# A hybrid decoder layer on one core: the first half of weight block 0 in two transfers of 256 columns, 256-wide first products, one warm-up product less

## The chip, the cores and the metric

The kernel runs on one core of a Trainium2 chip. The metric is device time in microseconds (us) for one execution; the time before is the median of three runs. Engines are named as the profile names them: PE (TensorE; PEld are its weight loads), DVE (VectorE), ACT (ScalarE), POOL (GpSimd), and SP (SyncE, which only issues transfers here). ACT issues a few transfers too; ACTq and SPq stand for the two queues.

## The reference

One decoder layer on 256 tokens of width 1024, all in float32: an input projection into two head groups (block-sparse attention and retention) with an output projection, cross-attention into a memory of 256 tokens, and a gated feed-forward block. Each has a normalised input and a normalised output that is added to x. Only the beginning matters here, the input projection:

```python
def rms_norm(x, g):
    xf = x.astype(jnp.float32)
    y = xf * lax.rsqrt(jnp.mean(xf * xf, axis=-1, keepdims=True) + NORM_EPS)
    return (y * g.astype(jnp.float32)).astype(x.dtype)
...
        h = rms_norm(x, g_pre_mix[l])
        proj = h @ w_in[l]
        mq, mk, mv, rq, rk, rv, rg = jnp.split(proj, SPLIT_POINTS, axis=-1)
```

## The kernel before

Every product is made of float32 operands split in two: a high part rounded to the matrix format (fp32r) and a low part, the rest. A product of x and w is then three products, high x with high w, low x with high w, high x with low w, all summed in one accumulator bank of 512 columns. The token-side scale of the norm is applied after the product, the gain before it.

The weights come in blocks of 128 x 1024 (512 KB) that SP loads in order of use into one of six `raw` tiles (`load_weight`, L149 to 157). ACT rounds a block into the high part (L197) and DVE subtracts for the low part (L198); both go into one of nine `hl` tiles. TensorE walks through a list of steps written out ahead, each with its products; side work is resumed between steps.

The opening is written out by hand, ahead of that list:

- TensorE starts with `WARM` products of constants (L999 and L1000), which feed nothing.
- ACT issues the transfer of the first half of block 0 (columns 0 to 511 of `raw0`, L989), then part 1 of x (`xr0`, L991), and loads its function table (L992).
- SP issues `xg` (L1014: the gains and part 0 of x), the second half of block 0 (L1015), the two halves of block 1 (L1016, L1017), parts 2 and 3 of x (L1018), and then whole blocks (L157).
- x is stored transposed in eight parts of 128 rows by 256 tokens. `gain_split` scales a part with the gain and rounds it on ACT (L230: high part of `xT`), then DVE makes the low part (L231).
- Block 0 has its own splitting (L1067 to 1078): DVE rounds the first half (L1074, CAST in the profile), ACT the second (L1077), DVE makes both low parts (L1078). Block 1 is split in halves by `split_weight(1, 2)`, after ACT has rounded part 1 of x.
- The first eight steps ("first", L1107 to 1116) multiply part q of x with half c of block q, q from 0 to 3. Each makes six products of 512 columns: three pairs of parts, each for both halves of the tokens. From block 4 on, steps are of the kind "col" (L1117 to 1133), with weights laid out in another way and the same three products (L1128 to L1130).

Transfers share eight completion counters (DMAHW0 to DMAHW7 in the order of instructions), given out in turn. A transfer that reuses a counter is issued only after the one before it on that counter has landed. A tile's reader waits for the transfer of just the columns that it reads.

Of the kernel before, what the change touches and what calls it, by code (L numbers as in the profile page):

```python
# [7 lines left out]
F32 = mybir.dt.float32  # L8
F32R = mybir.dt.float32r
BF16 = mybir.dt.bfloat16  # L10
AF = mybir.ActivationFunctionType
ALU = mybir.AluOpType
AX = mybir.AxisListType

P = 128
D = 1024
# [31 lines left out]
WARM = 9  # L48
# [7 lines left out]
def tile_hybrid_layer(  # L56
# [14 lines left out]
    nc = tc.nc  # L71
# [15 lines left out]
    def tok(t):  # L87
        return slice(t * P, (t + 1) * P)
# [33 lines left out]
    T = {}  # L122
# [866 lines left out]
    nc.scalar.dma_start(raws[0][:, 0:512], weights[0, :, 0:512])  # L989
    xr = [p4.tile([P, 4, 256], F32, tag="p4", name=f"xr{i}") for i in range(2)]  # L990
    nc.scalar.dma_start(xr[0][:, 1, :], gx[:, 288:544])  # L991
    nc.scalar.preload_act_table(AF.Exp)  # L992
# [20 lines left out]
    raws[1] = rawp.tile([P, D], F32, tag="raw", name="raw1")  # L1013
    nc.sync.dma_start(xg, gx[:, 0:288])  # L1014
    nc.sync.dma_start(raws[0][:, 512:1024], weights[0, :, 512:1024])  # L1015
    nc.sync.dma_start(raws[1][:, 0:512], weights[1, :, 0:512])  # L1016
# [54 lines left out]
    for c in range(2):  # L1071
        n = slice(c * 512, (c + 1) * 512)
        if c == 0:
            nc.vector.tensor_copy(hls[0][:, 0, n], raw[:, n])  # L1074
            gain_split("xT", 0, xg[:, 32:288], 0)
        else:
            nc.scalar.activation(hls[0][:, 0, n], raw[:, n], AF.Copy)  # L1077
        nc.vector.tensor_tensor(out=hls[0][:, 1, n], in0=raw[:, n], in1=hls[0][:, 0, n].bitcast(F32), op=ALU.subtract)  # L1078
# [9 lines left out]
    for i, s in enumerate(steps):  # L1088
# [17 lines left out]
        if s[0] == "first":  # L1106
# [4 lines left out]
            for a, (hx, hw) in enumerate(((0, 0), (1, 0), (0, 1))):  # L1111
                for t in range(2):
                    begin = q == 0 and a == 0
                    if begin:
                        accs[(c, t)] = accS(f"acc{c}{t}")
                    nc.tensor.matmul(accs[(c, t)], T["xT"][:, hx, q, tok(t)], h[:, hw, :], start=begin, stop=False)  # L1116
        elif s[0] == "col":  # L1117
# [5 lines left out]
            for kk in range(2):  # L1123
                k = 2 * kp + kk
                need((st, k, t))
                xh = T[st][:, 0, k, tok(t)]
                xl = T[st][:, 1, k, tok(t)]
                nc.tensor.matmul(acc, xh, h[:, 0, kk, :], start=(first and kk == 0), stop=False)  # L1128
                nc.tensor.matmul(acc, xh, h[:, 1, kk, :], start=False, stop=False)  # L1129
                nc.tensor.matmul(acc, xl, h[:, 0, kk, :], start=False, stop=(last and kk == 1))  # L1130
# [195 lines left out]
```

## Time and profile before

| what | value |
| --- | --- |
| median of 3 runs | 398.45 us |
| the three runs | 398.23, 398.45, 400.76 us |
| profiled execution | 398.61 us |
| its span, first to last instruction | 396.8 us |
| mean granted TensorE clock | 0.997 |
| bytes read from memory | 79.02 MB |

The span is what the profile covers, and the profiled execution's own time holds 1.8 us more around it. The trace gives starts and durations in us from the span's start. A row of the timeline or of the chain reads: start, duration, engine, line, operation, tiles written and read, shape, count, and in brackets how long the engine was idle before and what released it. A row of the view of waits reads: who waited, for whom, us in total, times, longest. In a table of issues the columns are tile, engine, count, KB each, and us from the issue to the landing. A row of grouped instructions has us busy and mean ns of one after the bar. Rows of stretches give busy us (and instructions) for PE, PEld, DVE, ACT and POOL, then the granted clock, the busy share of the 16 DMA engines, and GB/s.

### The profile page before, as it was taken

Reading aid. Unit: us, or ns where it says so; the run is one execution under the profiler, and the core shown is the slowest. Engines: PE = TensorE matmul, PEld = TensorE weight load, DVE = VectorE, ACT = ScalarE, POOL = GpSimd, SP = SyncE. Lnnn points to the kernel's source line nnn. Section 1 sums busy time; section 2 is a strip of 40 time slices with the busy share of each in tenths; the row PEclk is TensorE's granted clock in tenths of the full one; section 3 lists DMA queues with packets and bytes.
Section 4 is the critical chain, followed back from the end, with each engine's and each line's share of the span. In section 5 each row is a group of like instructions: output and inputs, shape, how many; then the busy total and the mean of one; then the engine's idle time right before and its main releaser. Section 6 shows DMA issues by size and latency. Waiting matters only on the chain.

```text
span 396.8 us, 5496 instructions
## 1 busy us (share of the span) xinstructions
PE 389.1 (98%) x1975; PEld 324.1 (82%) x1975; DVE 321.6 (81%) x448; ACT 259.7 (65%) x436; POOL 33.3 (8%) x53
## 2 busy tenths in 40 slices
PE   8999999999999999999999999999999999999993
PEld 4888787888889888888888888888888888888883
DVE  4865976785869977577576699999899799999964
ACT  5785965954767865494546866766758685656741
POOL 0010020200011000000001001013113103101000
PEclk9999999999999999999999999999999999999998
DMA  8998845568547676607272559779939878954102
GB/s 279 413 402 262 272 121 196 160 188 297 172 152 243 175 223 194 215 10 243 68 265 57 156 192 356 249 155 314 272 95 293 225 238 189 355 198 73 36 0 106
DMA packets 23067, 80.42 MB, mean 203 GB/s; under 512 B 2560, under 2 KB 3200, under 8 KB 23040
## 3 DMA queue, kind: packets, MB, share of 16 engines
q1 hardware_dynamic: 18144, 62.91, 46.6%
q0 software_dynamic: 4608, 16.78, 17.2%
q10 hardware_dynamic: 288, 0.39, 0.3%
q8 instruction: 15, 0.25, 0.3%
q14 instruction: 12, 0.10, 0.1%
HBM read 79.02 MB, written 1.05 MB: 202 GB/s over the span
## 4 chain that ended last, share of the span: by engine, by line
PE 89%; DVE 4%; ACT 3%; issue 2%; DMA 1%; POOLq 0%; POOL 0%; DVEq 0%; ACTq 0%
PE x L1192 11%; PE acc L1128 11%; PE acc L1129 10%; PE acc L1130 10%; PE acc L1152 9%; PE y L1192 5%; PE acc L1155 5%; PE down L1175 5%; PE down L1177 5%; PE down L1176 5%; PE acc L1116 3%; PE z L1192 3%; DVE hl L198 1%; ACT p_m L313 1%; DMA raw<-in_weights_dram 1%
## 5 line engine op out<-in xcount | busy, mean ns | idle before, releaser
L198 DVE TENSOR_TENSOR hl<-raw,hl 128x1024 fp32r<-128x1024 f32 (+1 forms) x102 | 119.4, 1188 | 16.9 <-ACT hl L197 16.6
L197 ACT ACTIVATE hl<-raw 128x1024 fp32r<-128x1024 f32 (+1 forms) x102 | 102.5, 1032 | 1.1 <-DMA raw<-in_weights_dram 0.9
L197 ACT ACTIVATE hl<-sum_qv 128x1024 fp32r<-128x1024 f32 x22 | 23.0, 1056 | 15.2 <-DVE sum_qv L204 12.2
L1128 PE MATMUL acc<-hl,xT 128*128 128x512 f32 x80 | 32.9, 411 | 0.1
L1175 PE MATMUL down<-hl,fT 128*128 128x512 f32 (+1 forms) x84 | 32.0, 381 | 0.0
L1176 PE MATMUL down<-hl,fT 128*128 128x512 f32 (+1 forms) x84 | 31.9, 380 | 0.0
L1177 PE MATMUL down<-hl,fT 128*128 128x512 f32 (+1 forms) x84 | 31.9, 380 | 0.0
L1130 PE MATMUL acc<-hl,xT 128*128 128x512 f32 x80 | 31.3, 392 | 0.0
L1129 PE MATMUL acc<-hl,xT 128*128 128x512 f32 x80 | 31.3, 391 | 0.0
L198 DVE TENSOR_TENSOR hl<-sum_kT,hl 128x1024 fp32r<-128x1024 f32 x24 | 29.0, 1220 | 1.4 <-ACT hl L197 1.3
L197 ACT ACTIVATE hl<-sum_kT 128x1024 fp32r<-128x1024 f32 x24 | 24.8, 1050 | 5.4 <-DVE sum_kT L204 3.5
L198 DVE TENSOR_TENSOR hl<-sum_qv,hl 128x1024 fp32r<-128x1024 f32 x22 | 26.6, 1218 | 1.3 <-ACT hl L197 1.3
L1192 PE MATMUL x<-hl,comb 128*128 128x512 f32 x96 | 23.2, 391 | 0.0
L1192 PE MATMUL x<-hl,x2T 128*128 128x512 f32 x96 | 23.2, 393 | 0.0
L1192 PE MATMUL y<-hl,comb 128*128 128x512 f32 x96 | 23.1, 389 | 0.0
L1192 PEld LDWEIGHTS x<-hl,comb 128*128 128x128 f32 x96 | 17.9, 188 | 4.0 <-DVE hl L198 0.3
L1192 PEld LDWEIGHTS y<-hl,comb 128*128 128x128 f32 x96 | 18.0, 188 | 3.7
L1192 PEld LDWEIGHTS x<-hl,x2T 128*128 128x128 f32 x96 | 17.8, 188 | 3.7
L1177 PEld LDWEIGHTS down<-hl,fT 128*128 128x128 f32 x84 | 15.8, 188 | 3.1 <-DVE fT L667 0.2
L1175 PEld LDWEIGHTS down<-hl,fT 128*128 128x128 f32 x84 | 15.8, 188 | 2.9
L1176 PEld LDWEIGHTS down<-hl,fT 128*128 128x128 f32 x84 | 15.8, 188 | 2.9
L1128 PEld LDWEIGHTS acc<-hl,xT 128*128 128x128 f32 x80 | 15.0, 188 | 3.8 <-issue 0.7
(257 smaller groups left out, 863.1 us busy)
## 6 DMA issues: line engine op xcount, KB each, us to landing
raw<-in_weights_dram SPq DMA_DIRECT2D x98, 512.0 KB, 4.9
sum_kT<-in_weights_dram POOLq DMA_DIRECT2D x14, 512.0 KB, 7.0
sum_qv<-in_weights_dram POOLq DMA_DIRECT2D x10, 512.0 KB, 5.8
sum_ret<-in_weights_dram POOLq DMA_DIRECT2D x8, 512.0 KB, 4.9
gpost<-in_gpost_dram SPq DMA_DIRECT2D x3, 512.0 KB, 4.5
x_sb<-in_x_dram SPq DMA_DIRECT2D x2, 512.0 KB, 8.2
memn<-in_mem_dram SPq DMA_DIRECT2D x2, 512.0 KB, 5.9
mr<-in_memT_dram SPq DMA_DIRECT2D x2, 512.0 KB, 7.4
```

The costliest lines, as they stand in the source:

```text
L197: nc.scalar.activation(h[:, 0, n], raw[:, n], AF.Copy)
L198: nc.vector.tensor_tensor(out=h[:, 1, n], in0=raw[:, n], in1=h[:, 0, n].bitcast(F32), op=ALU.subtract)
L1116: nc.tensor.matmul(accs[(c, t)], T["xT"][:, hx, q, tok(t)], h[:, hw, :], start=begin, stop=False)
L1128: nc.tensor.matmul(acc, xh, h[:, 0, kk, :], start=(first and kk == 0), stop=False)
L1129: nc.tensor.matmul(acc, xh, h[:, 1, kk, :], start=False, stop=False)
L1130: nc.tensor.matmul(acc, xl, h[:, 0, kk, :], start=False, stop=(last and kk == 1))
L1152: nc.tensor.matmul(acc, hls[q][:, 0, k * P:(k + 1) * P], T[f"{st}_k"][:, k, :], start=begin, stop=end, skip_group_check=True)
L1155: nc.tensor.matmul(acc[:, 0:256], hls[q][:, 1, k * P:(k + 1) * P], T[st][:, 0, k, :], start=begin, stop=end, skip_group_check=True)
L1175: nc.tensor.matmul(bank, fh, wh, start=first, stop=False, skip_group_check=True)
L1176: nc.tensor.matmul(bank, fh, wl, start=False, stop=False, skip_group_check=True)
L1177: nc.tensor.matmul(bank, fl, wh, start=False, stop=last, skip_group_check=True)
L1192: nc.tensor.matmul(acc, a, h[:, w, kk, :], start=begin and kk == 0 and n == 0, stop=end and n == 2, skip_group_check=True)
```

## The change

The transfer of the first half of block 0 is cut in two. Columns 0 to 255 stay first on ACT's queue; columns 256 to 511 become the second transfer on SP's queue, ahead of the second half. Block 1's first half moves from SP's queue to ACT's, as its third transfer. DVE rounds only columns 0 to 255, and ACT rounds columns 256 to 511; each piece has its low part made by itself. The first step's six products become ten: columns 0 to 255 with high and low weights, columns 256 to 511 with high weights, then low x with the high weights of all 512 columns, then columns 256 to 511 with low weights. `WARM` falls from 9 to 8. The "col" branch is written as a loop over the same three products.

```diff
-WARM = 9
+WARM = 8
...
-    nc.scalar.dma_start(raws[0][:, 0:512], weights[0, :, 0:512])
+    nc.scalar.dma_start(raws[0][:, 0:256], weights[0, :, 0:256])
     xr = [p4.tile([P, 4, 256], F32, tag="p4", name=f"xr{i}") for i in range(2)]
     nc.scalar.dma_start(xr[0][:, 1, :], gx[:, 288:544])
+    raws[1] = rawp.tile([P, D], F32, tag="raw", name="raw1")
+    nc.scalar.dma_start(raws[1][:, 0:512], weights[1, :, 0:512])
     nc.scalar.preload_act_table(AF.Exp)
...
-    raws[1] = rawp.tile([P, D], F32, tag="raw", name="raw1")
     nc.sync.dma_start(xg, gx[:, 0:288])
+    nc.sync.dma_start(raws[0][:, 256:512], weights[0, :, 256:512])
     nc.sync.dma_start(raws[0][:, 512:1024], weights[0, :, 512:1024])
-    nc.sync.dma_start(raws[1][:, 0:512], weights[1, :, 0:512])
     nc.sync.dma_start(raws[1][:, 512:1024], weights[1, :, 512:1024])
...
-    for c in range(2):
-        n = slice(c * 512, (c + 1) * 512)
-        if c == 0:
-            nc.vector.tensor_copy(hls[0][:, 0, n], raw[:, n])
-            gain_split("xT", 0, xg[:, 32:288], 0)
-        else:
-            nc.scalar.activation(hls[0][:, 0, n], raw[:, n], AF.Copy)
-        nc.vector.tensor_tensor(out=hls[0][:, 1, n], in0=raw[:, n], in1=hls[0][:, 0, n].bitcast(F32), op=ALU.subtract)
+    hi, lo = hls[0][:, 0], hls[0][:, 1]
+
+    def low_part(a, b):
+        nc.vector.tensor_tensor(out=lo[:, a:b], in0=raw[:, a:b], in1=hi[:, a:b].bitcast(F32), op=ALU.subtract)
+
+    nc.vector.tensor_copy(hi[:, 0:256], raw[:, 0:256])
+    low_part(0, 256)
+    gain_split("xT", 0, xg[:, 32:288], 0)
+    nc.scalar.activation(hi[:, 256:512], raw[:, 256:512], AF.Copy)
+    low_part(256, 512)
+    nc.scalar.activation(hi[:, 512:1024], raw[:, 512:1024], AF.Copy)
+    low_part(512, 1024)
...
-            for a, (hx, hw) in enumerate(((0, 0), (1, 0), (0, 1))):
+            if q == 0:
                 for t in range(2):
-                    begin = q == 0 and a == 0
-                    if begin:
-                        accs[(c, t)] = accS(f"acc{c}{t}")
-                    nc.tensor.matmul(accs[(c, t)], T["xT"][:, hx, q, tok(t)], h[:, hw, :], start=begin, stop=False)
+                    accs[(c, t)] = accS(f"acc{c}{t}")
+            a, b = slice(0, 256), slice(256, 512)
+            whole = slice(0, 512)
+            passes = [(0, 0, whole), (1, 0, whole), (0, 1, whole)]
+            if (q, c) == (0, 0):
+                passes = [(0, 0, a), (0, 1, a), (0, 0, b), (1, 0, whole), (0, 1, b)]
+            for hx, hw, n in passes:
+                for t in range(2):
+                    nc.tensor.matmul(accs[(c, t)][:, n], T["xT"][:, hx, q, tok(t)], h[:, hw, n],
+                                     start=(q == 0 and hx == 0 and hw == 0 and n is not b), stop=False, skip_group_check=True)
```

The first products on TensorE before: the last warm-up product, then the first step (accumulators `acc00` and `acc01`, one for each half of the tokens) up to the second step's `acc10`. In brackets stands the engine whose work a product waits for.

```order
L1000 MATMUL warm_105<-const-bfloat16-1.0 128x512
L1116 MATMUL acc00_155<-hl0_133,xT_118 128x512 [waits DVE_49,Activation_49]
L1116 MATMUL acc01_157<-hl0_133,xT_118 128x512
L1116 MATMUL acc00_155<-hl0_133,xT_118 128x512 [waits DVE_49]
...
L1116 MATMUL acc10_170<-hl0_133,xT_118 128x512 [waits Activation_49]
L1116 MATMUL acc11_172<-hl0_133,xT_118 128x512
```

The same place on TensorE now:

```order
L1002 MATMUL warm_107<-const-bfloat16-1.0 128x512
L1126 MATMUL acc00_157<-hl0_133,xT_119 128x256 [waits DVE_49,Activation_49]
L1126 MATMUL acc01_158<-hl0_133,xT_119 128x256
L1126 MATMUL acc00_157<-hl0_133,xT_119 128x256 [waits DVE_49]
...
L1126 MATMUL acc00_157<-hl0_133,xT_119 128x256 [waits Activation_49]
...
L1126 MATMUL acc00_157<-hl0_133,xT_119 128x512 [waits DVE_49]
L1126 MATMUL acc01_158<-hl0_133,xT_119 128x512
...
L1126 MATMUL acc10_176<-hl0_133,xT_119 128x512 [waits Activation_49]
L1126 MATMUL acc11_177<-hl0_133,xT_119 128x512
```

The low weights of columns 0 to 255 moved up to second place, and a wait for ACT (columns 256 to 511) came in at third place.

ACT's first instructions before: two transfers, the table load, then x and weights in turn.

```order
L989 DMA raw0_99<-in_weights_dram 128x512
L991 DMA xr0_101<-in_gx_dram 128x256
L992 ACT_TABLE_LOAD
L230 ACTIVATE xT_118<-xg_94 128x256 [waits DMAHW1_49]
L1077 ACTIVATE hl0_133<-raw0_99 128x512 [waits DMAHW2_49]
L230 ACTIVATE xT_118<-xr0_101,xg_94 128x256 [waits DMAHW3_49]
L197 ACTIVATE hl1_144<-raw1_120 128x512 [waits DMAHW4_49]
```

The same place on ACT now:

```order
L989 DMA raw0_99<-in_weights_dram 128x256
L991 DMA xr0_101<-in_gx_dram 128x256
L993 DMA raw1_104<-in_weights_dram 128x512
L994 ACT_TABLE_LOAD
L230 ACTIVATE xT_119<-xg_94 128x256 [waits DMAHW1_49]
L1080 ACTIVATE hl0_133<-raw0_99 128x256 [waits DMAHW3_49]
L1082 ACTIVATE hl0_133<-raw0_99 128x512 [waits DMAHW5_49]
L230 ACTIVATE xT_119<-xr0_101,xg_94 128x256 [waits DMAHW2_49]
L197 ACTIVATE hl1_146<-raw1_104 128x512 [waits DMAHW4_49]
```

A third transfer came in ahead of the table load, and a 256-wide rounding between x and the second half of block 0; the work behind it stands one place later.

SP's first instructions before:

```order
L1014 DMA xg_94<-in_gx_dram 128x288
L1015 DMA raw0_99<-in_weights_dram 128x512
L1016 DMA raw1_120<-in_weights_dram 128x512
L1017 DMA raw1_120<-in_weights_dram 128x512
L1018 DMA xr0_101<-in_gx_dram 128x512
L157 DMA raw2_126<-in_weights_dram 128x1024
L157 DMA raw3_128<-in_weights_dram 128x1024 [waits DMAHW0_49]
L1022 DMA xr1_102<-in_gx_dram 128x1024 [waits DMAHW1_49]
```

The same place on SP now:

```order
L1015 DMA xg_94<-in_gx_dram 128x288
L1016 DMA raw0_99<-in_weights_dram 128x256
L1017 DMA raw0_99<-in_weights_dram 128x512
L1018 DMA raw1_104<-in_weights_dram 128x512
L1019 DMA xr0_101<-in_gx_dram 128x512
L157 DMA raw2_126<-in_weights_dram 128x1024 [waits DMAHW0_49]
L157 DMA raw3_128<-in_weights_dram 128x1024 [waits DMAHW1_49]
L1023 DMA xr1_102<-in_gx_dram 128x1024 [waits DMAHW2_49]
```

The second half of block 0 went from second to third place, block 1's first half left the queue, and since eight transfers now go out ahead of block 2 instead of seven, block 2 waits for counter 0, which is that of the first weight transfer.

More of the change, by code (lines that the diff above doesn't have):

```diff
@@ L1127, in tile_hybrid_layer @@
                 xl = T[st][:, 1, k, tok(t)]
-                nc.tensor.matmul(acc, xh, h[:, 0, kk, :], start=(first and kk == 0), stop=False)
-                nc.tensor.matmul(acc, xh, h[:, 1, kk, :], start=False, stop=False)
-                nc.tensor.matmul(acc, xl, h[:, 0, kk, :], start=False, stop=(last and kk == 1))
+                for n, (a, w) in enumerate(((xh, 0), (xh, 1), (xl, 0))):
+                    nc.tensor.matmul(acc, a, h[:, w, kk, :], start=(first and kk == 0 and n == 0),
+                                     stop=(last and kk == 1 and n == 2), skip_group_check=True)
             if last:
```

## The prediction

> **What bounds the kernel now.** I read the page's busy shares and its chain by engine first, to see which engine a shift must go through. The profiled execution took 398.61 us: its span of 396.8 us and 1.8 us around it. It lies 0.16 us above the median of the runs shown, 398.45; the sum below is made against the profiled execution, and its difference is then put on the median.
>
> ```profile
> span 396.8 us, 5496 instructions
> PE 389.1 (98%) x1975; PEld 324.1 (82%) x1975; DVE 321.6 (81%) x448; ACT 259.7 (65%) x436; POOL 33.3 (8%) x53
> PE 89%; DVE 4%; ACT 3%; issue 2%; DMA 1%; POOLq 0%; POOL 0%; DVEq 0%; ACTq 0%
> ```
>
> TensorE is busy 98% of the span and carries 89% of the chain that ended last. So the opening is worth what it does to the time at which TensorE is through with it; from there a shift goes almost one for one to the end. Next the view of waits, for PE and its weight loads:
>
> ```profile
> PE acc L1116 <- DVE hl L1074: 0.8, 1, 0.8
> ...
> PEld acc L1116 <- ACT xT L230: 1.6, 1, 1.6
> ...
> PEld acc L1128 <- ACT rvd L242: 0.3, 1, 0.3
> ...
> PEld acc L1116 <- DVE hl L1078: 0.2, 1, 0.2
> ```
>
> The reader is to see that the first product has two gates which open almost together: the rounded weights (CAST, L1074) and the rounded x (L230). After it, the only wait of the opening is 0.2 us for the low part of the weights, and the largest later one 0.3 us, so little could swallow a shift. Then the timeline of the first microseconds (start, duration, engine, line; ACTq and SPq are transfers being issued):
>
> ```profile
> 0.74 0.41 ACTq L989 DMA_DIRECT2D raw<-in_weights_dram  x1
> 0.74 0.38 SPq L1014 DMA_DIRECT2D xg<-in_gx_dram  x1
> 0.78 4.00 PE L1000 MATMUL warm<-const-bfloat16-1.0 128*128 128x512 bf16 x9 [0.78 <-PEq L1316]
> 1.18 0.45 ACTq L991 DMA_DIRECT2D xr<-in_gx_dram  x1
> 1.18 0.42 SPq L1015 DMA_DIRECT2D raw<-in_weights_dram  x1
> 1.65 0.42 SPq L1016 DMA_DIRECT2D raw<-in_weights_dram  x1
> 1.66 1.28 ACT L992 ACT_TABLE_LOAD   x1 [1.66 <-PEq L1316]
> 2.12 0.43 SPq L1017 DMA_DIRECT2D raw<-in_weights_dram  x1
> 3.06 0.71 SPq L157 DMA_DIRECT2D raw<-in_weights_dram  x1
> 4.78 0.51 ACT L230 ACTIVATE xT<-xg 128x256 fp32r<-128x256 f32 x1 [1.84 <-DMA xg<-in_gx_dram]
> 4.96 0.43 DVE L1074 CAST hl<-raw 128x512 fp32r<-128x512 f32 x1 [4.96 <-DMA raw<-in_weights_dram]
> 5.33 0.48 DVE L231 SCALAR_TENSOR_TENSOR xT<-xg,xT 128x256 fp32r<-128x256 f32 x1
> 5.50 0.76 PEld L1116 LDWEIGHTS acc<-hl,xT 128*128 128x128 f32 x4 [1.64 <-ACT xT L230]
> 5.54 11.18 PE L1116 MATMUL acc<-hl,xT 128*128 128x512 f32 x48 [0.76 <-DVE hl L1074]
> 5.88 0.63 ACT L1077 ACTIVATE hl<-raw 128x512 fp32r<-128x512 f32 x1 [0.59 <-DMA raw<-in_weights_dram]
> 16.56 0.39 PE L1128 MATMUL acc<-hl,xT 128*128 128x512 f32 x1
> 22.00 0.39 PE L1128 MATMUL acc<-hl,xT 128*128 128x512 f32 x1
> ```
>
> And the issues with the us to landing (one view for each stretch in which they were issued; xg and the 4.2 one at 0.74, the 4.9 and 4.7 ones at 1.18, then 1.65, 2.12 and 3.06):
>
> ```profile
> xg<-in_gx_dram SPq DMA_DIRECT2D x1, 144.0 KB, 4.0
> raw<-in_weights_dram ACTq DMA_DIRECT2D x1, 256.0 KB, 4.2
> xr<-in_gx_dram ACTq DMA_DIRECT2D x1, 128.0 KB, 4.9
> raw<-in_weights_dram SPq DMA_DIRECT2D x1, 256.0 KB, 4.7
> ...
> raw<-in_weights_dram SPq DMA_DIRECT2D x1, 256.0 KB, 5.0
> ...
> raw<-in_weights_dram SPq DMA_DIRECT2D x1, 256.0 KB, 5.2
> ...
> raw<-in_weights_dram SPq DMA_DIRECT2D x1, 512.0 KB, 6.2
> ```
>
> Issue plus landing time gives the landings: xg 4.74, first half of block 0 4.93; second half of block 0 5.88, xr 6.08; first half of block 1 6.65, its second half 7.32; block 2 9.26. Two things follow. The last two halves land 0.67 us apart, so 256 KB cost 0.67 us once the queues run full. And the heads of the two queues land in pairs: 144 KB on SP with 256 KB on ACT (0.19 us apart), then 256 KB on SP with 128 KB on ACT (0.20 us apart). The smaller one is not ahead by its size. The nth transfer of one queue thus lands with the nth of the other, whatever its bytes.
>
> Last, the pace: 24 products from 16.56 to 22.00 are 5.44/24 = 0.227 us for one 512 wide. Blocks 1 to 3 have 36 such products before 16.56, so block 1 begins at 16.56 - 36 x 0.227 = 8.39. That time is what the change can move.
>
> **The change, step by step.**
>
> *First product.* Its gate of weights opens earlier, but the gate of x stays: xT's rounding ends at 4.78 + 0.51 = 5.29 and the weight load starts 0.21 later, at 5.50. Halving the ACT transfer alone would gain 5.54 - 5.50 = 0.04 us. What can gain more is that xg shares its way with 128 KB less. Bounds: nothing, and 128 KB at the pace above, 0.33 us. I take 0.30, since the pair lands together: xg at 4.44, first product at 5.24. CAST and low part of 256 columns follow their own landing (about 4.6) and fit ahead: for the nearest rows,
>
> ```profile
> L540 ACT ACTIVATE ckh<-kf 128x256 fp32r<-128x256 f32 x8 | 3.4, 430 | 0.2 <-DVE kf L741 0.2
> ...
> L541 DVE TENSOR_TENSOR ckl<-kf,ckh 128x256 fp32r<-128x256 f32 x8 | 3.3, 416 | 0.0
> ...
> 113.15 1.91 PE acc L1155 x16
> ```
>
> a 256-wide rounding on ScalarE takes 0.43 us, a low part on VectorE 0.42, and a 256-wide product 1.91/16 = 0.119 (chain of waits, whole group of 16). Even with a CAST of the full old 0.43 the low part ends at 4.6 + 0.43 + 0.42 = 5.45, by the third product (5.24 + 2 x 0.119 = 5.48) give or take 0.15.
>
> *Ten products in place of six.* 8 x 0.119 + 2 x 0.227 = 1.41 us against 6 x 0.227 = 1.36: 0.05 us, although each 256-wide product brings its own weight load.
>
> *Columns 256 to 512.* Their transfer is now the second on SP. The bytes through the second pair are 144 + 128 + 128 + 128 = 528 KB; before, 400 KB were there at 4.93 and 784 KB at 6.08, so between them 5.31. ScalarE rounds in 0.43 and TensorE starts some 0.2 later: 5.31 + 0.43 + 0.2 = 5.94, where TensorE would be ready at 5.24 + 4 x 0.119 = 5.72. A wait of 0.22 us, which takes the place of the old 0.2 us one. The group then ends at 5.94 + 4 x 0.119 + 2 x 0.227 = 6.87. The low part of these columns (0.42 us after 5.74) is there by 6.3, ahead of its products.
>
> *Columns 512 to 1024.* This is the step that decides. Their transfer was second on SP and is now third, and beside it, third on ACT, now runs block 1's first half. Bytes through the third pair: 528 + 256 + 256 = 1040 KB. The same 1040 KB were there before at 6.65 (block 1's first half). So the landing lies between 5.88, as before, and 6.65; I take 6.5, near the pair's end, for the pairing above. Rounding 0.63 and 0.2 to the first product: 7.33. TensorE is ready at 6.87 and waits 0.46 us; six products later, at 7.33 + 1.36 = 8.69, block 1 begins, against 8.39 before: **0.30 us later**. With a landing at 5.88 the rounding is through at 5.88 + 0.83 = 6.71; TensorE is ready at 6.87, or at 5.24 + 1.41 = 6.65 if columns 256 to 512 cost no wait, so block 1 begins between 8.07 and 8.23: 0.16 to 0.32 us earlier. With 6.65 it is 6.65 + 0.83 + 1.36 = 8.84: 0.45 us later.
>
> *Behind it.* ScalarE's x part 1 (0.5 us) and block 1's first half (0.63) follow the late rounding: 7.13 + 0.5 + 0.63 + 0.2 = 8.46, 0.2 us ahead of TensorE; VectorE's low parts are asked for only two to four products after that. One warm-up product less lies in idle time of TensorE. ACT's third issue (0.45, as its row for xr) moves the table load to end at 3.4, a microsecond before ScalarE is wanted. SP issues as many transfers as before, but block 2's issue, at 3.06, now waits for the first weight transfer (its counter is shared, see the order): about 4.65. With 4.0 us, the shortest landing seen, it lands at 8.65, and it did not land before 9.26 anyway, held by the bytes ahead. Nothing is paid.
>
> *Sum.* Profiled execution 398.61 + 0.30 = 398.9; on the median, 398.45 + 0.30 = 398.75, rounded to 398.8.
>
> **A clock that is not up yet.** Warm-up products come at a slower pace:
>
> ```profile
> 2.02 0.15 PEld L1000 LDWEIGHTS <-const-bfloat16-1.0 128*128 128x128 bf16 x1 [0.28 <-issue]
> ...
> 3.72 0.15 PEld L1000 LDWEIGHTS <-const-bfloat16-1.0 128*128 128x128 bf16 x1 [0.28 <-issue]
> ...
> 2.00:3.00 1.00, 1.00 (x4) 0.42 (x3) 0.00 (x0) 0.94 (x1) 0.00 (x0) 1.00 0.75 181
> ```
>
> Four steps from 2.02 to 3.72 are 0.425 us each for 512 columns, against 0.227 later; yet the clock column (1.00, third from the right) shows nothing of it. So the array rose from half pace between 3.72 and 5.54. Nine warm-ups keep it busy for 9 x 0.425 = 3.8 us, eight for 3.4. If eight don't suffice, the opening's products run at half pace for a while. The Trainium skill, "TensorE: Matmul & The Clock Gate", section "What's actually happening", says that a free-running window of about 3.4 us must have been busy before the clock is granted in full. By that, eight warm-ups would just fill one window that happened to begin with them, and nine have 0.4 us to spare; the trace of before fits it and can't show the threshold.
>
> **The rivals.**
>
> *Faster: the second half of block 0 isn't held up.* If the SP queue keeps its pace beside a third ACT transfer, block 1 begins 0.16 to 0.32 us earlier: 398.2. For it speaks that the DMA engines were only 0.75 busy from 2 to 3 us (second number from the right in the row above), so that more could run beside; against it, the pairing of landings. It decides if columns 512 to 1024 land before 8.39 - 1.36 - 0.83 = 6.2.
>
> *Slower: half pace in the opening.* Take the rise late by one run of nine warm-ups, 3.8 us from 5.24 to 9.04. The first group costs 8 x 0.213 + 2 x 0.425 = 2.55 and ends at 7.79, past the late rounding, whose wait vanishes. In the second group 3 products fall before 9.04 and 3 after: 3 x 0.425 + 3 x 0.227 = 1.96; block 1 begins at 9.75, 1.36 us later: 399.8. It decides if products after the first still come 0.2 us apart at 256 columns. Against it: in the trace the pace had risen by 5.54 with 0.8 us of idle time ahead of it.
>
> *Nothing happens.* xg lands at 4.74 again, and so does all else: the first product moves 0.04 us, and the time stays at 398.4. For it speaks that xg is its own transfer, first on its queue, and untouched.
>
> **How the numbers follow.** Forecast (0.1 to 0.45 us later) 0.5; faster rival 0.22; nothing 0.1; half pace 0.15; 0.03 for what I don't see. The range reaches from the faster rival at its bound (398.1), less the 0.2 us by which the fastest run lies under the median, to the half-pace rival (399.8) and the 0.16 us between profile and median: 397.9 to 400.0. 1% is 4.0 us, about what a measurement here can tell from no change, and no case comes near it in either direction: faster 0.01, same 0.97, slower 0.02.
>
> **What would show it.** In the profile after: xg landing near 4.4 and the first product near 5.24 (else the first term is wrong); ScalarE waiting for raw until about 6.5 ahead of the 512-wide rounding, and TensorE waiting some 0.46 us for it (else the pairing is); 256-wide products 0.12 us apart (0.21 is the half-pace rival); block 1 at 8.7. It is wrong as a whole if the time leaves the range while block 1 begins between 8.1 and 9.75: then the shift was not passed on one for one.

## The result and the profile after

The changed kernel took 401.23 us in the median of eight executions (400.32 to 402.39), the kernel before 398.51 us in eight beside it (398.04 to 400.76). The ratio is 1.0063, with a 95% interval of 1.004 to 1.0085: the change makes the kernel slower, by 2.7 us, where 0.3 us was forecast. The time lies outside the predicted range (397.9 to 400.0), though within 1%. The profiled execution took 400.46 us, 1.85 more than that of before.

The head of the page and its chain by engine, of the kernel after:

```profile
span 398.7 us, 5506 instructions
...
PE 388.7 (98%) x1978; PEld 324.4 (81%) x1978; DVE 321.4 (81%) x449; ACT 259.9 (65%) x437; POOL 33.3 (8%) x53
...
PE 88%; DVE 4%; ACT 3%; issue 2%; DMA 1%; SPq 0%; POOLq 0%; POOL 0%; DVEq 0%; ACTq 0%
```

TensorE has 0.4 us less work than before and yet the span is 1.9 us longer: the loss is waiting, not work. The view of waits, for PE and its weight loads:

```profile
PE acc L1126 <- ACT hl L1082: 1.9, 1, 1.9
...
PE acc L1126 <- ACT xT L230: 0.6, 1, 0.6
...
PEld acc L1126 <- ACT hl L1082: 2.1, 1, 2.1
```

One wait stands out, for ACT's rounding of columns 512 to 1024 (L1082). The timeline of the opening says why:

```profile
1.65 0.42 SPq L1017 DMA_DIRECT2D raw<-in_weights_dram  x1
1.65 0.45 ACTq L993 DMA_DIRECT2D raw<-in_weights_dram  x1
...
3.95 0.51 ACT L230 ACTIVATE xT<-xg 128x256 fp32r<-128x256 f32 x1 [0.53 <-DMA xg<-in_gx_dram]
4.13 0.29 DVE L1077 CAST hl<-raw 128x256 fp32r<-128x256 f32 x1 [4.13 <-DMA raw<-in_weights_dram]
...
4.57 1.81 PE L1126 MATMUL acc<-hl,xT 128*128 128x256 f32 x10 [0.62 <-ACT xT L230]
4.63 0.42 ACT L1080 ACTIVATE hl<-raw 128x256 fp32r<-128x256 f32 x1 [0.17 <-DMA raw<-in_weights_dram]
...
7.58 0.63 ACT L1082 ACTIVATE hl<-raw 128x512 fp32r<-128x512 f32 x1 [2.54 <-DMA raw<-in_weights_dram]
...
8.26 0.96 PE L1126 MATMUL acc<-hl,xT 128*128 128x512 f32 x3 [1.88 <-ACT hl L1082]
...
17.90 6.28 PE L1140 MATMUL acc<-hl,xT 128*128 128x512 f32 x27
```

The first product starts at 4.57, 0.97 us earlier than before (5.54), and the ten products of the first step are through at 6.38. Then nothing until 8.26, because ACT is idle for 2.54 us ahead of L1082, waiting for the transfer. The first product of the "col" steps, which stood at 16.56, stands at 17.90: 1.34 us later. Two issues at the same moment, 1.65, carry it; in the view of issues (KB each, us to landing) they are

```profile
raw<-in_weights_dram SPq DMA_DIRECT2D x1, 256.0 KB, 5.9
raw<-in_weights_dram ACTq DMA_DIRECT2D x1, 256.0 KB, 6.1
```

Columns 512 to 1024 land at 1.65 + 5.9 = 7.55, block 1's first half at 7.75: a pair, as forecast, but the first of them 0.9 us later than the upper bound of 6.65. The DMA engines' busy share and GB/s (the last two numbers) of two stretches, in the kernel after:

```profile
3.50:5.50 2.00, 1.38 (x8) 0.86 (x7) 1.33 (x4) 0.93 (x2) 0.00 (x0) 1.00 0.53 160
5.50:7.50 2.00, 0.89 (x6) 0.58 (x4) 0.12 (x1) 0.00 (x0) 0.00 (x0) 1.00 1.00 330
```

and in the kernel before:

```profile
3.50:5.50 2.00, 1.28 (x3) 0.15 (x1) 0.54 (x2) 0.51 (x1) 0.00 (x0) 1.00 0.97 350
5.50:7.50 2.00, 1.97 (x9) 1.54 (x10) 1.86 (x4) 1.62 (x4) 0.00 (x0) 1.00 1.05 397
```

From 3.5 to 5.5 us the engines were full before and are half idle in this execution. From 3.5 to 7.5 us they moved 2 x 350 + 2 x 397 = 1494 KB before and 2 x 160 + 2 x 330 = 980 KB after.

The rest of the loss lies at the other end of the kernel. The chain's piece called "issue 4.78", in which TensorE finishes the last products, starts 1.38 us later, but the span is 1.9 us longer. SP's waits from 390 us on, before:

```profile
SPq L1322 <- DMA out_dram<-x_sb: 1.4, 2, 1.1
```

and after:

```profile
SPq L1333 <- DMA out_dram<-x_sb: 1.8, 1, 1.8
```

What SP does at that line behind the last such wait (semaphore instructions, their durations in ns, first and last start), before:

```profile
L1322 SPq EVENT_SEMAPHORE  x3: 17/17/28, 395.9 to 396.8; - x3
```

and after:

```profile
L1333 SPq EVENT_SEMAPHORE  x10: 17/28/28, 397.3 to 398.6; - x10
```

At the end SP waits for the transfers' eight counters one after another. The transfers take the counters in turn, and the kernel after has one transfer more in all. Before, the last output transfer sat on the counter that is waited for last, so that the other seven were passed during its flight. After, it sits on an earlier one, and seven more instructions come behind its landing. From the start of the issue of the last output transfer to the start of SP's last instruction, just before the span ends, pass 3.14 us before and 3.58 after: 0.44 us. With 1.38 that makes 1.82 of the 1.85 us between the two profiled executions.

### The profile page after: what moved, and what is told of

Same layout as the page of the kernel before. It is cut to its first block, busy times and chain, and to the rows that moved or that the text cites. A ratio compares the mean times of both kernels' runs of the same rounds, so it can differ in the third digit from the quotient of the medians.

```text
span 398.7 us, 5506 instructions
## 1 busy us (share of the span) xinstructions
PE 388.7 (98%) x1978; PEld 324.4 (81%) x1978; DVE 321.4 (81%) x449; ACT 259.9 (65%) x437; POOL 33.3 (8%) x53
## 4 chain that ended last, share of the span: by engine, by line
PE 88%; DVE 4%; ACT 3%; issue 2%; DMA 1%; SPq 0%; POOLq 0%; POOL 0%; DVEq 0%; ACTq 0%
PE acc L1140 31%; PE x L1203 11%; PE acc L1163 9%; PE y L1203 5%; PE acc L1166 5%; PE down L1188 5%; PE down L1186 5%; PE down L1187 5%; PE z L1203 3%; PE acc L1126 2%; DMA raw<-in_weights_dram 1%; DVE hl L198 1%; ACT p_m L313 1%; PE c_f L664 1%; ACT hl L197 1%
## 5 line engine op out<-in xcount | busy, mean ns | idle before, releaser
L1140 PE MATMUL acc<-hl,xT 128*128 128x512 f32 x240 | 59.4, 398 | 0.1
L1140 PEld LDWEIGHTS acc<-hl,xT 128*128 128x128 f32 x240 | 43.8, 188 | 9.8 <-issue 0.7
L1140 PE MATMUL acc<-hl,memT 128*128 128x512 f32 x96 | 23.0, 392 | 0.0
L1140 PE MATMUL acc<-hl,oT 128*128 128x512 f32 x96 | 22.9, 392 | 0.0
L1140 PE MATMUL acc<-hl,x2T 128*128 128x512 f32 x96 | 22.5, 392 | 0.0
L1140 PE MATMUL acc<-hl,mixT 128*128 128x512 f32 x96 | 22.2, 390 | 0.0
L1140 PEld LDWEIGHTS acc<-hl,mixT 128*128 128x128 f32 x96 | 17.9, 188 | 3.9 <-issue 0.2
L1140 PEld LDWEIGHTS acc<-hl,x2T 128*128 128x128 f32 x96 | 17.9, 188 | 3.7
```

Of the source, the lines that this page charges most:

```text
L1140: nc.tensor.matmul(acc, a, h[:, w, kk, :], start=(first and kk == 0 and n == 0), stop=(last and kk == 1 and n == 2), skip_group_check=True)
```

## The experiments

The theory is that the late landing of columns 512 to 1024, held up by the third transfer on ACT's queue, is the main loss. Its rival puts the loss on the clock: eight warm-up products in place of nine. Later came two more questions, what the additional transfer costs at the end, and what about the third ACT transfer delays the landing. All times are medians beside the kernel before on the same chip.

**Nine warm-ups again.** The kernel after with

```diff
-WARM = 8
+WARM = 9
```

> The changed kernel with nine warm-up products again. If the loss beyond the profiled opening comes from the clock falling during TensorE's long wait for columns 512 to 1024, the ninth product, which lies ahead of that wait, changes nothing: 401.2 us within 0.5, and single runs still spread over 2 us. If the missing product itself is the cause, the time comes back by 0.8 us or more, to 400.4 or below, with runs close together.

400.68 us (400.26 to 401.23, 4 executions) against 398.25, ratio 1.0058 [1.0043, 1.0073]. The time lies between the two expectations, and the runs spread over 1 us, not 2. Of the 2.7 us 2.4 stay: the warm-up is not the main part of the loss. Columns 512 to 1024 land at 1.64 + 5.8 = 7.44. Whether the ninth product gives something back can't be told, since its profiled execution began at half pace all the same. Its stretches for PE (busy us and products, clock, DMA share, GB/s):

```profile
6.50:7.50 1.00, 1.00 (x5) 1.00 0.95 326
7.50:8.50 1.00, 1.00 (x4) 1.00 0.92 336
8.50:9.50 1.00, 1.00 (x3) 1.00 0.97 381
9.50:10.50 1.00, 1.00 (x6) 1.00 1.03 360
```

Four and then three products in a us that was busy throughout, then six: TensorE was at half pace until about 9.5. That is the half-pace rival of the prediction, with nine warm-ups, and as worked out there the wait for the late rounding vanishes behind it.

**Block 1's first half back on SP.** The kernel after, with this transfer in fourth place on SP:

```diff
-    nc.scalar.dma_start(raws[1][:, 0:512], weights[1, :, 0:512])
...
     nc.sync.dma_start(raws[0][:, 512:1024], weights[0, :, 512:1024])
+    nc.sync.dma_start(raws[1][:, 0:512], weights[1, :, 0:512])
```

> The changed kernel with block 1's first half back on SP's queue (xg, columns 256 to 511, columns 512 to 1023, then block 1). Theory 1 (the third transfer of a queue reaches the DMA engines late, and the narrow transfers ahead of it are through too soon to cover that): columns 512 to 1024 land no earlier than 6.9, TensorE waits over 1.2 us, 400 us or more. Theory 2 (block 1's half on ACT takes half of the bandwidth): they land by 6.2, TensorE waits under 0.4 us, 398.5 us or less.

398.89 us (398.18 to 399.31, 10 executions) against 398.25, ratio 1.0012 [1.0003, 1.0022]. Of 2.7 us 0.6 are left, so this one transfer, with what follows from it, makes up 2.1. The timeline and the stretch, to be set beside those of after:

```profile
6.07 0.63 ACT L1082 ACTIVATE hl<-raw 128x512 fp32r<-128x512 f32 x1 [0.96 <-DMA raw<-in_weights_dram]
...
6.75 3.03 PE L1126 MATMUL acc<-hl,xT 128*128 128x512 f32 x12 [0.31 <-ACT hl L1082]
```

```profile
3.50:5.50 2.00, 1.35 (x8) 0.80 (x7) 1.28 (x4) 0.93 (x2) 0.00 (x0) 1.00 0.86 274
```

Columns 512 to 1024 land at 1.64 + 4.4 = 6.04, 1.5 us earlier than in after, with the place on SP's queue unchanged; the DMA engines are busier, and TensorE waits 0.3 us. The theory of the landing holds: it is the transfer beside it on ACT, not the third place on SP. The time is 0.4 us over the 398.5 that was expected for this case, about what the additional transfer costs at the end (below).

**Columns 512 to 1024 second, 256 to 511 third.** The kernel after with the two SP transfers exchanged:

```diff
-    nc.sync.dma_start(raws[0][:, 256:512], weights[0, :, 256:512])
     nc.sync.dma_start(raws[0][:, 512:1024], weights[0, :, 512:1024])
+    nc.sync.dma_start(raws[0][:, 256:512], weights[0, :, 256:512])
```

> The changed kernel with columns 512 to 1023 second and columns 256 to 511 third on SP's queue. Theory 1: the second transfer lands about 5.0, the third, now 128 KB, not before 6.3, and TensorE waits for it in the middle of its first step: block 1 begins about 9.2 (6.3 + 0.43 + 0.2 + 0.94 + 1.36), 399.3 us or more. Theory 2: both have landed by 5.7, block 1 begins near 8.5, about 398.6 us.

403.32 us (402.65 to 404.38, 4 executions) against 398.25, ratio 1.0121 [1.0098, 1.0144]. Now columns 512 to 1024 land at 1.18 + 3.8 = 4.98, and columns 256 to 511, half the size but third, land at 1.65 + 5.7 = 7.35. The third place beside ACT's third is what is late, whatever its own bytes. Engines that stand idle are not needed for it, since they were 0.99 busy here (second number from the right):

```profile
3.50:5.50 2.00, 1.45 (x6) 0.59 (x4) 1.12 (x3) 0.51 (x1) 0.00 (x0) 1.00 0.99 286
```

TensorE waits four products into the first step (start, duration, line):

```profile
4.56 0.87 PE L1126 MATMUL acc<-hl,xT 128*128 128x256 f32 x4 [0.48 <-ACT xT L230]
...
7.85 4.64 PE L1126 MATMUL acc<-hl,xT 128*128 128x256 f32 x12 [2.42 <-ACT hl L1080]
```

and the clock falls meanwhile (third number from the right):

```profile
6.00:7.00 1.00, 0.00 (x0) 0.00 (x0) 0.00 (x0) 0.00 (x0) 0.00 (x0) 1.00 0.99 335
7.00:8.00 1.00, 0.15 (x1) 0.15 (x1) 0.17 (x1) 0.62 (x2) 0.00 (x0) 0.54 1.02 373
8.00:9.00 1.00, 1.00 (x4) 0.90 (x5) 0.91 (x3) 1.00 (x3) 0.00 (x0) 0.50 1.00 401
...
13.00:14.00 1.00, 1.00 (x4) 0.75 (x4) 1.00 (x3) 0.63 (x3) 0.00 (x0) 0.55 1.01 410
14.00:15.00 1.00, 1.00 (x6) 0.83 (x5) 0.64 (x2) 0.97 (x1) 0.00 (x0) 1.00 1.04 418
```

During 2.4 us without products the granted clock falls to half, from about 7.1 to 13.9. So a wait can cost more than its length.

**Eight warm-ups alone.** The kernel before with

```diff
-WARM = 9
+WARM = 8
```

> The kernel before with eight warm-up products, nothing else changed. If eight suffice for the clock, the products of the first step still come 0.23 us apart and the time is 398.5 us within 0.3. If eight are too few, the opening runs at half pace for up to 3.8 us and the time is 399.0 to 400.0 us.

398.52 us (397.92 to 400.16, 10 executions) against 398.25, ratio 1.0015 [1.0, 1.0029]. Seven of the ten lie below 398.8, three at 399.81, 400.08 and 400.16; of 19 executions of the kernel before in the same session none was above 399.07, though one of the eight beside the changed kernel took 400.76. So eight warm-ups mostly cost nothing, and sometimes about what the half-pace rival was priced at; nine don't rule out such an execution. No trace was taken of one of the three, so that it is the clock there is an inference.

**One transfer more, far from the opening.** The kernel before with a table of constants, needed late, loaded in two pieces:

```diff
-        nc.sync.dma_start(cst[:, :C_DEC], consts[:, :C_DEC])
+        nc.sync.dma_start(cst[:, :C_MCOS], consts[:, :C_MCOS])
+        nc.sync.dma_start(cst[:, C_MCOS:C_DEC], consts[:, C_MCOS:C_DEC])
```

> The kernel before with one more transfer, far from the opening (the table of constants loaded in two pieces). Theory: the last output transfer moves on to another of the eight counters, which SP's closing sequence checks second instead of last, so that seven more checks of about 0.06 us follow its landing. From the issue of the last output transfer to the end 3.6 us instead of 3.2, time 0.4 us over that of before. Rival: the 0.45 us at the end come from the opening in some other way; then this kernel takes the time of before within 0.15 us.

399.0 us (398.38 to 399.37, 11 executions) against 398.33, ratio 1.0013 [1.0005, 1.0022]. The ratio puts the time 0.5 us over before (0.2 to 0.9), where 0.4 was expected. From the issue of the last output transfer to SP's last instruction pass 3.57 us, where the kernel before has 3.14, and behind the landing SP has ten instructions again:

```profile
L1323 SPq EVENT_SEMAPHORE  x10: 17/28/28, 396.1 to 397.4; - x10
```

One additional transfer costs 0.43 us at the end, here as in the opening. In every kernel of this study with as many transfers as before, the stretch takes 3.13 or 3.14 us; with one more, 3.56 to 3.58; with two more, 3.50.

**Only block 1's first half moved to ACT.** The kernel before with its 512-column transfers, and

```diff
     nc.scalar.dma_start(xr[0][:, 1, :], gx[:, 288:544])
+    raws[1] = rawp.tile([P, D], F32, tag="raw", name="raw1")
+    nc.scalar.dma_start(raws[1][:, 0:512], weights[1, :, 0:512])
...
-    raws[1] = rawp.tile([P, D], F32, tag="raw", name="raw1")
-    nc.sync.dma_start(raws[1][:, 0:512], weights[1, :, 0:512])
```

> The kernel before with only block 1's first half moved to ACT's queue as its third transfer. Theory 1 (third transfers on both queues at once are fed slowly, whatever their widths): the DMA engines' busy share falls to 0.7 or less between 4.5 and 6.5 us, block 1's halves land at 7.3 or later (before: 6.65 and 7.32), TensorE waits for block 1 for up to 0.5 us; columns 512 to 1024, second on SP, land near 5.9 as before. Theory 2 (only narrow transfers ahead leave the hole): no hole, landings within 0.3 us of before, time within 0.3 us.

398.52 us (397.82 to 399.62, 10 executions) against 398.33, ratio 1.0008 [0.9999, 1.0017]: no difference that is measured. The second half of block 0, second on SP as before, lands early enough for its rounding to start at 5.31; ACT's third transfer still lands at 1.65 + 5.9 = 7.55, and SP's third, block 1's second half, at 1.65 + 5.7 = 7.35. The stretch:

```profile
3.50:5.50 2.00, 1.79 (x4) 0.65 (x3) 1.09 (x3) 0.70 (x2) 0.00 (x0) 1.00 1.07 390
```

So each theory came half true: the engines stay full, and yet the third pair lands at 7.3 or later. By 7.55 the 1296 KB of three pairs are through here; in the kernel after the 1040 KB of three pairs are through at 7.75. The 256 KB fewer ahead brought the third pair no earlier. Here nothing urgent is in it: block 1 is wanted late. In these kernels the third ACT transfer does harm only when the urgent one stands beside it.

**The wait filled with products.** The kernel after with seven more products of constants between the first and the second step. They feed nothing:

```diff
+            if (q, c) == (0, 0):
+                for _ in range(7):
+                    nc.tensor.matmul(warm, one(P), one(512), start=True, stop=True)
```

> The changed kernel with seven products of constants (512 wide, results unused) between its first and second step, where TensorE waits 1.9 us. If the spread of the changed kernel's runs (400.3 to 402.4 us) is the clock falling during that wait, the products (7 x 0.23 = 1.6 us, less than the wait) keep it up: median 400.4 us, all runs within 0.8 us of each other. If the spread has another cause, it stays at 2 us and the median at 401.2.

400.6 us (399.89 to 402.2, 6 executions) against 398.33, ratio 1.0058 [1.0039, 1.0076]. The median is near the 400.4 of the falling clock, the spread of 2.3 us is that of its rival. The spread of after is still there, so a clock that falls in the wait can't be its only source. What share it has stays open.

**A version that might have beaten both.** ACT loads columns 0 to 255 and then 256 to 511, and nothing more; SP loads xg, columns 512 to 1024, part 1 of x, then block 1; nine warm-ups, and x itself, needed late, in one transfer in place of two, so that the total is that of before.

```diff
-    nc.scalar.dma_start(xr[0][:, 1, :], gx[:, 288:544])
+    nc.scalar.dma_start(raws[0][:, 256:512], weights[0, :, 256:512])
...
-    nc.scalar.dma_start(raws[1][:, 0:512], weights[1, :, 0:512])
...
-    nc.sync.dma_start(raws[0][:, 256:512], weights[0, :, 256:512])
     nc.sync.dma_start(raws[0][:, 512:1024], weights[0, :, 512:1024])
+    nc.sync.dma_start(xr[0][:, 1, :], gx[:, 288:544])
+    nc.sync.dma_start(raws[1][:, 0:512], weights[1, :, 0:512])
...
-        for t in range(2):
-            nc.sync.dma_start(x_sb[:, t, :], x[tok(t), :])
+        nc.sync.dma_start(x_sb, x.rearrange("(t p) d -> p t d", p=P))
```

> Two transfers on ACT's queue (columns 0 to 255, 256 to 511 of block 0), all others on SP's in the order xg, columns 512 to 1023, x part 1, block 1; nine warm-up products; x loaded in one transfer, so that the number of transfers is that of before. No queue's third transfer is asked for early, the wait for columns 512 to 1024 goes: first product near 4.7, block 1 begins near 8.0 against 8.39 before, the end as in before: 397.9 us. Rival: the first product of before comes as early in some executions, and the time is that of before within 0.2 us.

398.51 us (398.24 to 399.82, 12 executions) against 398.33, ratio 1.0007 [0.9998, 1.0015]. Its profiled execution starts the first product at 4.58, has no wait on PE after it in the opening, and reaches the "col" products at 16.30, 0.26 us ahead of before's. But before's opening varies by as much: it reaches them at 16.08 in the profile with eight warm-ups alone and at 16.35 in that with one transfer more. In the times nothing of the gain shows, and of all versions here none is faster than the kernel before.

**Eight KB in third place on ACT.** The kernel with block 1's first half on SP, and 16 columns of the gains loaded third on ACT into a tile that nobody reads:

```diff
+    tiny = cpool.tile([P, 16], F32, tag="tiny", name="tiny")
+    nc.scalar.dma_start(tiny, gx[:, 0:16])
```

> The kernel b1_on_sp (block 1's first half on SP's queue) with one extra third transfer on ACT's queue of 8 KB in rows of 64 B, which nothing reads. If columns 512 to 1024 are late because a third transfer on ACT's queue holds up the feeding of SP's, its bytes don't matter: they land at 7.0 or later, the DMA engines are less than 0.8 busy between 3.5 and 5.5 us, and the time is 400 us or more. If they are late because of the bytes of the transfer beside them, they land at 6.0 to 6.2 as in b1_on_sp, and the time is that of b1_on_sp (398.9) plus at most 0.1.

399.14 us (398.99 to 400.11, 6 executions) against 398.21, ratio 1.0028 [1.0017, 1.0039]. Columns 512 to 1024 land at 1.64 + 4.5 = 6.14, against 6.04 without it. A third transfer as such delays nothing that can be told; its bytes do. The time lies 0.25 us above that with block 1 on SP, where at most 0.1 was expected. The profiled execution waits 0.6 us at 11.84 for the rounding of block 2. With one transfer more ahead, parts 2 and 3 of x wait for a shared counter and block 2 is issued behind them, at 4.57 in place of 4.18; it lands at 4.57 + 6.6 = 11.17, in place of 4.18 + 5.3 = 9.48 with block 1 on SP. Whether that makes the difference in the other executions isn't shown.

**The landing alone.** The kernel after with nine warm-ups, the same seven products in the wait, and x in one transfer:

```diff
-WARM = 8
+WARM = 9
...
-        for t in range(2):
-            nc.sync.dma_start(x_sb[:, t, :], x[tok(t), :])
+        nc.sync.dma_start(x_sb, x.rearrange("(t p) d -> p t d", p=P))
...
+            if (q, c) == (0, 0):
+                for _ in range(7):
+                    nc.tensor.matmul(warm, one(P), one(512), start=True, stop=True)
```

> The changed kernel with nine warm-up products, the seven products of constants in its long wait, and x loaded in one transfer (the number of transfers of before). The late landing stays, the two clock losses and the 0.43 us at the end go: block 1 about 1.4 us later than in before, time 1.4 us over before (399.7), at most one run in four over 400.4. If the late landing alone makes up the whole loss, the time stays at 401.

399.79 us (399.48 to 401.38, 6 executions) against 398.21, ratio 1.0044 [1.0029, 1.0059]. Columns 512 to 1024 land at 7.55 again, and the end takes 3.14 us. So the late landing, together with the 256-wide pieces and the ten products, is worth about 1.6 us. The next run has the pieces and the ten products without the late landing and lies 0.45 us over before, so the landing itself is worth between 1.1 and 1.6.

**Everything but the landing.** The kernel after with block 1's first half on SP, nine warm-ups, and x in one transfer:

```diff
-WARM = 8
+WARM = 9
...
-    nc.scalar.dma_start(raws[1][:, 0:512], weights[1, :, 0:512])
...
+    nc.sync.dma_start(raws[1][:, 0:512], weights[1, :, 0:512])
...
-        for t in range(2):
-            nc.sync.dma_start(x_sb[:, t, :], x[tok(t), :])
+        nc.sync.dma_start(x_sb, x.rearrange("(t p) d -> p t d", p=P))
```

> The kernel b1_on_sp with nine warm-up products and x loaded in one transfer. All three causes are undone (late landing, fewer warm-up products, one transfer more), while the 256-wide pieces and the ten products stay: the time of before within 0.3 us. If the pieces themselves cost something, it is 0.5 us or more over before.

398.66 us (398.29 to 399.27, 11 executions) against 398.21, ratio 1.0009 [1.0, 1.0017]. That is 0.45 us over before, more than the 0.3 that was expected and less than the 0.5 that would have charged the pieces. The interval reaches down to 1.0. All three cures together bring the kernel back to near where it was; what the rest is stays open. In its profile columns 512 to 1024 land at 1.65 + 4.0 = 5.65.

**Half of it.** The kernel after with 256 columns of block 1 third on ACT and the next 256 fourth on SP:

```diff
-    nc.scalar.dma_start(raws[1][:, 0:512], weights[1, :, 0:512])
+    nc.scalar.dma_start(raws[1][:, 0:256], weights[1, :, 0:256])
...
+    nc.sync.dma_start(raws[1][:, 256:512], weights[1, :, 256:512])
```

> The changed kernel with only columns 0 to 255 of block 1 (128 KB) as ACT's third transfer; its columns 256 to 511 go fourth on SP's queue. If the delay goes with the bytes beside them, columns 512 to 1024 land halfway between b1_on_sp and the changed kernel, about 6.8, and the time is about 400. If any third transfer of a size that matters stops the feeding, they land at 7.3 or later.

399.71 us (399.14 to 400.23, 5 executions) against 398.26, ratio 1.0034 [1.0021, 1.0047]. The columns land about where the first theory had them (6.8), and the rounding (timeline) and the stretch lie between those with block 1 on SP and those of after:

```profile
6.98 0.63 ACT L1083 ACTIVATE hl<-raw 128x512 fp32r<-128x512 f32 x1 [1.61 <-DMA raw<-in_weights_dram]
```

```profile
3.50:5.50 2.00, 1.87 (x7) 1.01 (x5) 1.22 (x4) 0.93 (x2) 0.00 (x0) 1.00 0.73 224
```

| third on ACT | columns 512 to 1024 land at | DMA share, 3.5 to 5.5 us |
| --- | --- | --- |
| nothing (block 1 on SP; everything but the landing) | 6.04; 5.65 | 0.86; 0.91 |
| 8 KB | 6.14 | 0.89 |
| 128 KB | 6.94 | 0.73 |
| 256 KB (after; nine warm-ups; wait filled; landing alone; behind the table load) | 7.55; 7.44; 7.35; 7.55; 7.55 | 0.53; 0.67; 0.78; 0.78; 0.65 |

The landing goes with the bytes on ACT, and repeats within 0.4 us. The share of the engines doesn't go with it in the same way: at 0.73 the columns landed at 6.94, at 0.78 at 7.35 and 7.55. So how empty the engines stand is not what sets the landing.

**Behind the table load.** The kernel after with ACT's third transfer written after the load of the function table:

```diff
-    nc.scalar.dma_start(raws[1][:, 0:512], weights[1, :, 0:512])
     nc.scalar.preload_act_table(AF.Exp)
+    nc.scalar.dma_start(raws[1][:, 0:512], weights[1, :, 0:512])
```

> The changed kernel with ACT's third transfer issued after the table load, 1.3 us later (near 3 us instead of 1.65). If the delay needs both third transfers at the same moment, columns 512 to 1024 land at 6.0 to 6.4 and the engines are over 0.8 busy from 3.5 to 5.5 us; block 1's first half then lands near 8 and TensorE waits for it instead. If it only matters that ACT has a third transfer of 256 KB at all, they land at 7.0 or later.

400.91 us (400.24 to 401.34, 4 executions) against 398.26, ratio 1.0064 [1.0046, 1.0081]. The edit did not move the issue: it still starts at 1.69, so the load doesn't hold up the transfer behind it, and the landing stays at 7.55. It repeats after, and whether a later issue would help was not tried otherwise. Its profile shows something else, the first step at half pace with eight warm-ups:

```profile
4.55 2.52 PE L1126 MATMUL acc<-hl,xT 128*128 128x256 f32 x10 [0.20 <-ACT xT L230]
```

The ten products take 2.52 us in place of after's 1.81. The half-pace rival had put them at 2.55. The wait for the late rounding hides it: TensorE waits 1.2 us in place of 1.9, and the next step starts at 8.29, where after's starts at 8.26.

## Why the prediction was wrong

- **Columns 512 to 1024: the step that failed.** The pairing of the nth transfers and the direction were right, and the price was not. The prediction put the landing between 5.88 and 6.65, since "the same 1040 KB were there before at 6.65". That takes it that the bytes arrive at before's pace, whatever the order. In the kernel after the landing was 7.55. The 256 KB beside it, 0.67 us at full pace, cost 7.55 - 6.04 = 1.5 us (1.3 to 1.9 over the profiles of the table), and half of them 0.9. TensorE's wait is 1.9 us in place of 0.46, and the "col" products come 1.34 us later in place of 0.30. Without the other effects the time grows by 1.1 to 1.6 us. Why a third pair lands this late is not settled. The engines stood half idle in one profile (0.53 between 3.5 and 5.5 us, 0.97 before), but they were 0.78 busy in another with the same landing, and full where 256 KB transfers stood ahead, with a third pair that landed no earlier.
- **The end of the kernel: a missing term.** "SP issues as many transfers as before ... Nothing is paid" counted one queue. Over both queues it is one more, and that moves the last output transfer to another counter, which costs 0.43 us at the end. The prediction had the shared counters at the start of the kernel only. The runs with and without an additional transfer show it.
- **The first product: wrong on the cautious side.** It started at 4.57, not 5.24, since xg landed at 0.74 + 3.2 = 3.94, not 4.44. The bounds 4.41 to 4.74 came from one execution. With xg's neighbours unchanged, it landed after 3.3, 3.3 and 3.5 us in three other profiles, where before's shows 4.0. With the smaller neighbour of after and nine warm-ups it landed after 3.9. So that the smaller neighbour brings xg forward, the reason for the 0.30 us, is not shown. The lead was worth nothing here, as the wait behind swallowed it.
- **Ten products in place of six, and the wait for columns 256 to 511: right, where the pace was up.** 1.81 us for the step in place of 1.41 + 0.22 = 1.63. The columns landed at 1.18 + 3.4 = 4.58, and ACT started on them 0.17 us after its rounding of x, so they held nothing up for longer than forecast.
- **The warm-up in idle time: right in most executions only.** Seven of ten lost nothing with eight warm-ups, three about 1.6 us. The half-pace rival had 15% and a price of 399.8; the three lie at 399.8 to 400.2. But it also came in the profiled execution with nine. And it came with eight in the profile with the transfer behind the table load (2.52 us for ten products), where the late rounding hid it. By the windows of the Trainium skill, "TensorE: Matmul & The Clock Gate", section "What's actually happening", where the window falls decides; that this was so in these executions no run shows.
- **ACT's table load and block 2's later issue: nothing was paid, in part by luck.** No wait of the opening names either. But block 2 landed at 4.13 + 6.1 = 10.23, not at 9.26; TensorE itself was 1.34 us late by then.
- **Passed on one for one: right.** 1.34 us at the "col" products are 1.38 at the end of TensorE's work. The sign that was named for the contrary did come: block 1 began at 17.90 - 36 x 0.227 = 9.73, between 8.1 and 9.75, and the time left the range. Its conclusion doesn't follow, since the sign had no room for a loss at the end of the kernel. That 9.73 is close to the half-pace rival's 9.75 is chance; the products of this profile were not at half pace.

The sum against the profiled execution is 1.38 + 0.44 = 1.82 of 1.85 us. Against the median, 2.7 us, 1.1 to 1.6 and 0.4 leave 0.7 to 1.2. The profiled execution is among the three shortest of its eight. The two longest, 402.35 and 402.39, have the lowest mean clocks, 0.992 and 0.993 against 0.997, and 0.0045 x 399 = 1.8 us is about what separates them from it. That speaks for a clock that falls in the wait, as in the kernel with columns 512 to 1024 second. Against it stand an execution of 400.32 at 0.994, and one of 402.2 at 0.997 among those with the wait filled. How the rest divides between a clock that rises late, one that falls again, and the pieces stays open.

## What to carry to other kernels

A transfer that is put beside an urgent one can't be priced from when the same bytes were through before: 1040 KB were there at 6.65 in one order and at 7.75 in the other. The landing is taken from a trace that has this order, or its bound allows for twice the price at full pace and more (1.3 to 1.9 us here, in place of 0.67). Count the transfers of all queues when one is split, since where the last one falls among the shared counters can cost as much as the edit was to gain. And a landing from one profile needs a second one beside it before it bounds anything: xg's varied by 0.7 us between kernels that load it in the same way.

## What the runs showed of the hardware

- A wait of 2.42 us on TensorE, behind 0.87 us of products, was enough, in the profiled execution with columns 512 to 1024 second, for the granted clock to be halved for 6.8 us (about 7.1 to 13.9). The Trainium skill, "TensorE: Matmul & The Clock Gate", section "What's actually happening", names one idle window of about 3.4 us for it; 6.8 us are two such windows, but the gap that set it off was shorter than one.
- The clock column stands at 1.00 while a half-pace start lasts (the rows of nine warm-ups), and does show a later fall. The pace at the start is read from the products counted in a stretch.
- A 256 KB transfer that stands third on ACT landed after 5.9 to 6.1 us in each of the seven kernels that have one, whether 128 or 256 KB stood ahead and whether the engines were 0.53 or 1.07 busy from 3.5 to 5.5 us.
